# The spreading products of the norms, ranked 120 places later in a two-layer trunk

## The chip, the cores and the metric

The kernel runs as one program on one core of one Trainium2 chip. The metric is the device time of one execution in microseconds, the median of several runs. Before the change it is 2375.06 us (three runs, 2371.31 to 2375.71).

## What is computed

One step of a trunk of two layers over 1032 token columns (1024 of a prompt and 8 samples), width 1024, in float32. Layer 0 mixes by a gated recurrence and a causal convolution whose output has a LayerNorm of its own; layer 1 mixes by a short gated convolution. After every mixer and after every feed-forward block (width 2816) comes a post-norm:

```python
def _layernorm(x, w, b):
    mu = jnp.mean(xf, axis=-1, keepdims=True)
    var = jnp.mean(jnp.square(xf - mu), axis=-1, keepdims=True)
    return (xf - mu) * lax.rsqrt(var + LN_EPS) * w + b

# odd layer
p = x @ w_in                       # three parts bg, cg, xv
z = cg * xv
y = (bg * _causal_dwconv(z_ext, conv_w)) @ w_out
x = _layernorm(ALPHA * x + y)
# both layers
f = (silu(x @ w1) * (x @ w3)) @ w2
x = _layernorm(ALPHA * x + f)
```

## The kernel before

The channels lie on the partitions, the tokens along the free axis, in three chunks of 384, 384 and 264 columns (numbers 0, 1 and 2). A chunk's running state is `r` (eight slices of 128 channels). For the matrix products every operand is split in a high and a low part by `split` (L119 to L121): ScalarE casts the high part (L120), VectorE subtracts it from the source (L121). Weights come by SyncE's DMAs in units of 128 x 1024 (`raw`, 512 KB) and are split into `wh` and `wl`; activations are split into `x0ha, x0la, x0hb, x0lb` (chunk 0, slices 0 to 3 and 4 to 7), the same with `x1` for chunk 1, `x2h, x2l` for chunk 2, and `hb` for the hidden units of a feed-forward block. `mm` (L141 to L150) multiplies one unit by one chunk: for each of eight slices three matmuls (L147 `wl` by the high part, L148 `wh` by the low part, L149 `wh` by the high part) into one PSUM tile. They are called large matmuls here; they are nearly all of TensorE's work. Some projections of chunks 0 and 1 run through a scheme with fewer products (`project`), whose operands `t2`, `t3` are made on VectorE (L691 to L705).

A norm is the generator `normalise` (L220 to L270). It sums the slices on VectorE, spreads the mean by one TensorE product (L230), subtracts it (L241), squares on ScalarE (L248), sums (L250, L253), brings the sum of squares to the partitions by 4 or 3 small products with one column each (L256), scales it on VectorE (L201) and raises it to the power -0.5 on POOL (L202). This gives `rs`, one factor per token, with the tokens on the partitions. Then 4 (3 for chunk 2) small products spread it over all partitions (L265): `rs`, broadcast, by the identity, 96 columns each (88 for chunk 2), each in two passes in the profile. They write one tile of the PSUM pool `sm` (three buffers). VectorE multiplies the four pairs of slices by it (L268), and the affine step follows (L280 on VectorE for slice 0, L282 on ScalarE for the others), then the splits into `x?h`, `x?l`, which the next large matmuls read. The norm of the convolution in layer 0 goes the same way with two pairs and ends in L568 to L570 and in the splits of `x1` or `x2`.

There are 15 norms, in the order of the program: 1 the convolution of chunk 0; 2 the mixer's norm of chunk 0; 3 and 4 the convolutions of chunks 1 and 2; 5 and 6 the mixer's norms of chunks 1 and 2; 7, 8, 9 the feed-forward norms of layer 0 (chunks 0, 1, 2); 10, 11, 12 the mixer's norms of layer 1; 13, 14, 15 the final norms.

The order of each engine's instructions is set when the program is built, by a scheduler of tiles: an instruction takes the place that its number `tc.cur_priority` gives it. The number grows as the code is written, so that what is written later stands later, as far as dependences and buffers allow. The code raises or lowers the number by hand at a few places (`LATER = 1500` around the convolution, L556 to L559). On the chip each engine works through its fixed order and waits where an operand is not there.

Of the kernel before, what the change touches and what calls it, by code (L numbers as in the profile page):

```python
# [48 lines left out]
HC_BUFS = 24  # L49
TP_BUFS = 4  # L50
LATER = 1500
DVE_AFFINE = (0,)
DVE_AFFINE_LAST = (5, 6, 7)

# [14 lines left out]
def trunk(ctx: ExitStack, tc: tile.TileContext, xT, win0, wout0, win1, wout1, w1, w3, w2, vecs, sh, scf, ssc,  # L69
# [127 lines left out]
    def col(i):  # L197
        return vec[:, i:i + 1]

    def rsqrt_small(dst, src, scale, eps, n, p=P):  # L200
        VE.tensor_scalar(dst, src, scale, eps, ALU.mult, ALU.add)  # L201
        GP.tensor_tensor(dst, dst, mhalf[:p, :n], ALU.pow)  # L202
# [17 lines left out]
    def normalise(pairs, w, onesm, denom, last=False):  # L220


        acc = lnp.tile([P, 2, 384], F32, name="acc")
        mu = smp.tile([P, 512], F32, name="sm")[:, :w]
        n = len(pairs) - last
        VE.tensor_tensor(acc[:, :, :w], pairs[0], pairs[1], ALU.add)
        for v2 in pairs[2:n]:
            VE.tensor_tensor(acc[:, :, :w], acc[:, :, :w], v2, ALU.add)
        VE.tensor_tensor(acc[:, 0, :w], acc[:, 0, :w], acc[:, 1, :w], ALU.add)
        PE.matmul(mu, onesm, acc[:, 0, :w], start=True, stop=not last)  # L230
        if last:
            VE.tensor_tensor(acc[:, 1, :w], pairs[-1][:, 0], pairs[-1][:, 1], ALU.add)
            PE.matmul(mu, onesm, acc[:, 1, :w], start=False, stop=True)
        yield
        nb = 4 if w == 384 else 3
        bw = w // nb
        st = smp.tile([P, 512], F32, name="sm")
        rs = lnp.tile([P, 4], F32, name="rs")
        acc2 = lnp.tile([P, 2, 384], F32, name="acc")
        for j, v2 in enumerate(pairs):  # L240
            VE.tensor_tensor(v2, v2, mu.unsqueeze(1).broadcast_to([P, 2, w]), ALU.subtract)  # L241
            if j == 0:
                sq = acc2
            elif last and j == 2:
                sq = lnp.tile([P, 2, 384], F32, name="acc")
            else:
                sq = lnp.tile([P, 2, 384], F32, name="sq", bufs=1)
            SC.square(sq[:, :, :w], v2)  # L248
            if j and not last:
                VE.tensor_tensor(acc2[:, :, :w], acc2[:, :, :w], sq[:, :, :w], ALU.add)  # L250
            if last or j == len(pairs) - 1:
                z = sq if last else acc2
                VE.tensor_tensor(z[:, 0, :w], z[:, 0, :w], z[:, 1, :w], ALU.add)  # L253
                for i in range(nb):
                    k = 4 * i + j if last else i
                    PE.matmul(st[:bw, k:k + 1], z[:, 0, i * bw:(i + 1) * bw], ones, start=True, stop=True)  # L256
        var = st[:bw, :nb]
        if last:
            var = rs[:bw, :nb]
            VE.tensor_reduce(var, st[:bw, :4 * nb].rearrange("p (i j) -> p i j", j=4), mybir.AxisListType.X, ALU.add)  # L260
        rsqrt_small(rs[:bw, :nb], var, 1.0 / denom, LN_EPS, nb, bw)
        yield
        pb = smp.tile([P, 512], F32, name="sm")[:, :w]
        for i in range(nb):
            PE.matmul(pb[:, i * bw:(i + 1) * bw], rs[:bw, i:i + 1].broadcast_to([bw, P]), ident[:bw, :bw],  # L265
                      start=True, stop=True)
        for j, v2 in enumerate(pairs):
            VE.tensor_tensor(v2, v2, pb.unsqueeze(1).broadcast_to([P, 2, w]), ALU.mult)  # L268
            if j % 2:
                yield  # L270

    def layer_norm(c, wi, bi, out=None):
        a, b = CH[c]
        view = rc[c]
        last = out is not None and c == 2
        yield from normalise([view[:, j:j + 2, :] for j in range(0, NK, 2)], b - a, on1k, D, last)
        for k in range(NK):
            v = view[:, k, :]
            if k in (DVE_AFFINE_LAST if last else DVE_AFFINE):
                VE.tensor_scalar(v, v, col(wi + k), col(bi + k), ALU.mult, ALU.add)  # L280
            else:
                SC.activation(v, v, AF.Identity, bias=col(bi + k), scale=col(wi + k))  # L282
            if out is None:
                split(*xp(k, c), v)
            elif k % 2:
                nc.sync.dma_start(out[:, NK * a:NK * b].rearrange("p (k t) -> p k t", k=NK)[:, k - 1:k + 1, :],
                                  view[:, k - 1:k + 1, :])
            if k % 2:
                yield
# [47 lines left out]
    with tc.tile_pool(name="hg", bufs=1) as hg, tc.tile_pool(name="hg2", bufs=2) as hg2:  # L337
# [169 lines left out]
        def conv(i, gs, u, acc):  # L507

            w = sum(CH[g][1] - CH[g][0] for g in gs)
            W = w - NS if 2 in gs else w  # L510
            VE.tensor_scalar(acc[:, :w], u[:, 30:30 + w], col(V_DW + 30 * 4 + i), col(V_DWB + i), ALU.mult, ALU.add)
            for d in range(1, KW):
                lo = d if gs[0] == 0 else 0
                VE.scalar_tensor_tensor(acc[:, lo:W], u[:, 30 + lo - d:30 + W - d], col(V_DW + (30 - d) * 4 + i),  # L514
                                        acc[:, lo:W], ALU.mult, ALU.add)
            if 2 in gs:
                st = hg.tile([P, NS, 30], F32, name="stc", tag="vm")
                nc.sync.dma_start(st, scf[i])
                nw = hg.tile([P, NS, 30], F32, name="ncs", tag="S0t")
                SC.copy(nw[:, :, 0:29], st[:, :, 1:30])  # L520
                SC.copy(nw[:, :, 29], u[:, 30 + W:30 + W + NS])
                nc.sync.dma_start(cs_o[i], nw)
                nc.sync.dma_start(cp_o[i], u[:, W:W + 30])
                dw = vec[:, V_DW:V_DW + 120].rearrange("p (j i) -> p i j", i=4)[:, i, :]
                VE.tensor_tensor(st, st, dw.unsqueeze(1).broadcast_to([P, NS, 30]), ALU.mult)
                ts = hg.tile([P, NS], F32, name="tcs")
                VE.tensor_reduce(ts, st, mybir.AxisListType.X, ALU.add)
                VE.tensor_tensor(acc[:, W:W + NS], acc[:, W:W + NS], ts, ALU.add)

        def conv_units(i, gs):  # L530
# [25 lines left out]
            p = tc.cur_priority  # L556
            tc.cur_priority = p + LATER
            conv(i, gs, u_t, ctile[gs, i // 2][:, i % 2, :])
            tc.cur_priority = p  # L559

        def conv_finish(g):
            w = CH[g][1] - CH[g][0]
            pairs = [ctile[g, j] for j in range(2)]
            yield from normalise(pairs, w, on512, 512)
            for i in range(4):
                v = pairs[i // 2][:, i % 2, :]
                sg = hg2.tile([P, 384], F32, name="ct")[:, :w]
                SC.activation(sg, v, AF.Sigmoid, bias=col(V_CLB + i), scale=col(V_CLW + i))  # L568
                SC.activation(v, v, AF.Identity, bias=col(V_CLB + i), scale=col(V_CLW + i))
                VE.tensor_tensor(v, v, sg, ALU.mult)  # L570
                put_y(4 + i, g, v)
                if i % 2:
                    yield
# [247 lines left out]
    with tc.tile_pool(name="t0", bufs=1, reuse_waits="tile") as tp:  # L821
        F0.T = {j: t_pair(tp, j) for j in (2, 3)}
        with tc.tile_pool(name="head0", bufs=1, reuse_waits="tile") as act:
# [6 lines left out]
            for m in range(0, NEARLY, 4):  # L830
# [4 lines left out]
                p = tc.cur_priority  # L835
# [117 lines left out]
    with tc.tile_pool(name="t1", bufs=1, reuse_waits="tile") as tp:  # L953
        F1.T = {j: t_pair(tp, j) for j in (2, 3)}
        with tc.tile_pool(name="head1", bufs=1, reuse_waits="tile") as act:
# [12 lines left out]
            p = tc.cur_priority  # L968
# [81 lines left out]
```

## Time and profile before

| what | before |
|---|---|
| median of 3 runs | 2375.06 us (2371.31 to 2375.71) |
| the profiled execution | 2371.57 us |
| its span in the profile | 2369.5 us |
| TensorE busy | 2311.5 us, 98% |
| VectorE busy | 1789.8 us, 76% |
| ScalarE busy | 903.6 us, 38% |
| POOL busy | 42.8 us, 2% |

The span runs from the first to the last instruction; the execution is 2.1 us longer. TensorE's busy time counts overlapping, pipelined matmuls, so the distance between the starts of two matmuls says what one costs, and the length of a row does not. Where a row waited, the time and what released it stand in brackets.

### The profile page before, as it was taken

Reading aid. Unit: us, or ns where it says so; the run is one execution under the profiler, and the core shown is the slowest. Engines: PE = TensorE matmul, PEld = TensorE weight load, DVE = VectorE, ACT = ScalarE, POOL = GpSimd, SP = SyncE. Lnnn points to the kernel's source line nnn. Section 1 sums busy time; section 2 is a strip of 40 time slices with the busy share of each in tenths; the row PEclk is TensorE's granted clock in tenths of the full one; section 3 lists DMA queues with packets and bytes.
Section 4 is the critical chain, followed back from the end, with each engine's and each line's share of the span. In section 5 each row is a group of like instructions: output and inputs, shape, how many; then the busy total and the mean of one; then the engine's idle time right before and its main releaser. Section 6 shows DMA issues by size and latency. Waiting matters only on the chain.

```text
span 2369.5 us, 36483 instructions
## 1 busy us (share of the span) xinstructions
PE 2311.5 (98%) x14866; PEld 2272.3 (96%) x14866; DVE 1789.8 (76%) x2980; ACT 903.6 (38%) x1504; POOL 42.8 (2%) x40
## 2 busy tenths in 40 slices
PE   9999999999899999999999899999999999999997
PEld 8999999999899999999999899999999999999997
DVE  8998888787863336777788888877857777777775
ACT  5434353335631223332355333444513332332552
POOL 0000000000000000000000000000000000000000
PEclk9999999999999999999999999999999999999998
DMA  5322322343341221222442233434402222224651
GB/s 190 115 79 73 97 78 69 116 161 115 116 125 45 80 73 48 69 81 65 154 147 73 63 107 106 120 116 147 119 19 72 79 72 63 63 81 125 206 194 46
DMA packets 86999, 235.03 MB, mean 99 GB/s; under 512 B 8384, under 2 KB 26560, under 8 KB 86576
## 3 DMA queue, kind: packets, MB, share of 16 engines
q1 hardware_dynamic: 86672, 232.26, 32.0%
q8 instruction: 116, 1.90, 0.3%
q0 software_dynamic: 160, 0.45, 0.1%
q14 instruction: 51, 0.42, 0.1%
HBM read 225.46 MB, written 7.21 MB: 98 GB/s over the span
## 4 chain that ended last, share of the span: by engine, by line
PE 89%; DVE 6%; ACT 2%; POOL 1%; issue 1%; DMA 1%; SPq 0%; POOLq 0%; DVEq 0%; ACTq 0%
PE mm L147 20%; PE mm L149 20%; PE mm L148 20%; PE mm L656 8%; PE mm L657 8%; PE mm L655 8%; PE sm L368 2%; DVE wl L121 1%; DVE cc L514 1%; POOL rs L202 1%; PE sm L265 1%; ACT wh L120 1%; ACT r L282 0%; PE sm L415 0%; PE sm L397 0%
## 5 line engine op out<-in xcount | busy, mean ns | idle before, releaser
L120 ACT CAST wh<-raw 128x1024 fp32r<-128x1024 f32 (+1 forms) x494 | 493.3, 1001 | 898.2 <-PE mm L149 530.1
L121 DVE TENSOR_TENSOR wl<-raw,wh 128x1024 fp32r<-128x1024 f32 (+1 forms) x494 | 572.7, 1161 | 152.5 <-ACT wh L120 148.4
L147 PE MATMUL mm<-x2h,wl 128*128 128x264 f32 x1216 | 351.5, 289 | 20.5 <-DVE wl L121 20.5
L149 PE MATMUL mm<-x2h,wh 128*128 128x264 f32 x1216 | 349.6, 287 | 0.0
L148 PE MATMUL mm<-x2l,wh 128*128 128x264 f32 x1216 | 348.8, 287 | 0.0
L147 PEld LDWEIGHTS mm<-x2h,wl 128*128 128x128 f32 x1216 | 232.4, 191 | 23.0 <-DVE wl L121 22.6
L296 DVE TENSOR_TENSOR r<-r,mm 128x384 f32<-128x384 f32 (+1 forms) x336 | 171.2, 521 | 96.8 <-PE mm L149 96.2
L148 PEld LDWEIGHTS mm<-x2l,wh 128*128 128x128 f32 x1216 | 232.5, 191 | 0.3
L149 PEld LDWEIGHTS mm<-x2h,wh 128*128 128x128 f32 x1216 | 231.8, 191 | 0.8 <-issue 0.8
L147 PE MATMUL mm<-hb,wl 128*128 128x384 f32 (+1 forms) x672 | 211.1, 319 | 2.4 <-ACT hb L120 2.3
L148 PE MATMUL mm<-hb,wh 128*128 128x384 f32 (+1 forms) x672 | 213.2, 319 | 0.0
L149 PE MATMUL mm<-hb,wh 128*128 128x384 f32 (+1 forms) x672 | 212.3, 318 | 0.0
L514 DVE SCALAR_TENSOR_TENSOR cc<-r,vec,cc 128x640 f32<-128x640 f32 (+19 forms) x240 | 172.5, 737 | 1.2
L147 PEld LDWEIGHTS mm<-hb,wl 128*128 128x128 f32 x672 | 125.0, 188 | 4.7 <-ACT hb L120 4.7
L148 PEld LDWEIGHTS mm<-hb,wh 128*128 128x128 f32 x672 | 126.2, 188 | 0.5 <-DVE hb L121 0.2
L149 PEld LDWEIGHTS mm<-hb,wh 128*128 128x128 f32 x672 | 126.3, 188 | 0.3
L147 PE MATMUL mm<-x0ha,wl 128*128 128x384 f32 x312 | 108.3, 348 | 6.8 <-DVE wl L121 6.8
L148 PE MATMUL mm<-x0la,wh 128*128 128x384 f32 x312 | 108.0, 346 | 0.8 <-DVE x0la L121 0.8
L149 PE MATMUL mm<-x0ha,wh 128*128 128x384 f32 x312 | 108.5, 348 | 0.0
L149 PE MATMUL mm<-x0hb,wh 128*128 128x384 f32 x312 | 108.0, 346 | 0.0
L147 PE MATMUL mm<-x0hb,wl 128*128 128x384 f32 x312 | 107.4, 344 | 0.0
L148 PE MATMUL mm<-x0lb,wh 128*128 128x384 f32 x312 | 107.0, 343 | 0.0
(320 smaller groups left out, 5425.4 us busy)
## 6 DMA issues: line engine op xcount, KB each, us to landing
raw<-in_w SPq DMA_DIRECT2D x256, 512.0 KB, 3.6
raw<-in_win SPq DMA_DIRECT2D x98, 512.0 KB, 3.7
raw<-in_wout SPq DMA_DIRECT2D x48, 512.0 KB, 3.6
raw<-in_w SPq DMA_DIRECT2D x16, 256.0 KB, 2.6
out_yT<-r SPq DMA_DIRECT2D x8, 384.0 KB, 3.0
S0t<-in_sh SPq DMA_DIRECT2D x8, 256.0 KB, 3.4
out_hs<-S0t SPq DMA_DIRECT2D x8, 256.0 KB, 2.0
r<-in_xT SPq DMA_DIRECT2D x4, 384.0 KB, 6.7
```

Source lines behind the costliest of these rows:

```text
L120: SC.copy(hi, src)
L121: VE.tensor_tensor(lo, src, hi.bitcast(F32), ALU.subtract)
L147: PE.matmul(ps, wl[:, k, :], h, start=k == 0, stop=False)
L148: PE.matmul(ps, wh[:, k, :], l, start=False, stop=False)
L149: PE.matmul(ps, wh[:, k, :], h, start=False, stop=k == kt - 1)
L202: GP.tensor_tensor(dst, dst, mhalf[:p, :n], ALU.pow)
L296: VE.tensor_tensor(v, v, ps, ALU.add)
L368: PE.matmul(ps[:sr, c * 64:(c + 1) * 64].rearrange("p (b i) -> p b i", i=hh), kp[:, c * P:c * P + sr], qr, start=True, stop=True)
L514: VE.scalar_tensor_tensor(acc[:, lo:W], u[:, 30 + lo - d:30 + W - d], col(V_DW + (30 - d) * 4 + i), acc[:, lo:W], ALU.mult, ALU.add)
L655: PE.matmul(ps, w[1][:, k], t[0][:, k], start=k == 0, stop=False)
L656: PE.matmul(ps, w[0][:, k], t[1][:, k], start=False, stop=False)
L657: PE.matmul(ps, w[0][:, k], t[0][:, k], start=False, stop=k == 3)
```

## The change

The spreading products of L265 are ranked 120 places later than the code around them: the priority number is raised before the loop and set back after it. What follows them in the code (L268 and on) keeps its own number, but needs their result.

```diff
@@ constants
 LATER = 1500
+FACTOR_LATER = 120
@@ normalise
         rsqrt_small(rs[:bw, :nb], var, 1.0 / denom, LN_EPS, nb, bw)
         yield
         pb = smp.tile([P, 512], F32, name="sm")[:, :w]
+        p = tc.cur_priority
+        tc.cur_priority = p + FACTOR_LATER
         for i in range(nb):
             PE.matmul(pb[:, i * bw:(i + 1) * bw], rs[:bw, i:i + 1].broadcast_to([bw, P]), ident[:bw, :bw],
                       start=True, stop=True)
+        tc.cur_priority = p
         for j, v2 in enumerate(pairs):
             VE.tensor_tensor(v2, v2, pb.unsqueeze(1).broadcast_to([P, 2, w]), ALU.mult)
```

In the changed code the lines after the edit have other numbers: the spreading product is L268 there (L265 before), the multiplication L272 (L268), the variance product L257 (L256), the three large matmuls L148 to L150 (L147 to L149), the split L122 (L121).

The groups of norms 3, 4 and 7 to 14 (10 of 15, 37 products) stand elsewhere in TensorE's order; those of 1, 2, 5, 6 and 15 stay. Most lie 35 to 95 rows later, and single products now alternate with large matmuls, where a block of three or four stood before. POOL's order is the same. On VectorE the multiplications and splits that hang on the group stand later, behind weight splits and other work. On SyncE the load of a small state tile goes behind one more weight load, and the output transfers of norms 13 and 14 behind several.

TensorE around the variance and spreading products of norm 4 (convolution of chunk 2), before. `x1ha` to `x1lb` are chunk 1's operands:

```order
L256 MATMUL sm<-ones,acc 88x1 x3
L147 MATMUL mm<-x1ha,wl 128x384
L148 MATMUL mm<-x1la,wh 128x384
L149 MATMUL mm<-x1ha,wh 128x384
L147 MATMUL mm<-x1hb,wl 128x384
L148 MATMUL mm<-x1lb,wh 128x384
L149 MATMUL mm<-x1hb,wh 128x384
L147 MATMUL mm<-x1hb,wl 128x384
L148 MATMUL mm<-x1lb,wh 128x384
L265 MATMUL sm<-ident,rs 128x88 x3
```

And after the change:

```order
L257 MATMUL sm<-ones,acc 88x1 x3
L148 MATMUL mm<-x1ha,wl 128x384
L149 MATMUL mm<-x1la,wh 128x384
L150 MATMUL mm<-x1ha,wh 128x384
L268 MATMUL sm<-ident,rs 128x88
L148 MATMUL mm<-x1ha,wl 128x384
L268 MATMUL sm<-ident,rs 128x88
L149 MATMUL mm<-x1la,wh 128x384
L268 MATMUL sm<-ident,rs 128x88
L150 MATMUL mm<-x1ha,wh 128x384
```

Before, eight large matmuls stood between the variance products and the spreading products; now three do, since the variance products moved further than the spreading ones.

TensorE before the first products on chunk 2 after norm 12 (mixer's norm of chunk 2, layer 1), after the change. `x2h` is chunk 2's high operand, which that norm writes:

```order
L268 MATMUL sm<-ident,rs 128x88
L148 MATMUL mm<-x1hb,wl 128x384
L268 MATMUL sm<-ident,rs 128x88
L149 MATMUL mm<-x1lb,wh 128x384
L268 MATMUL sm<-ident,rs 128x88
L150 MATMUL mm<-x1hb,wh 128x384
L148 MATMUL mm<-x1hb,wl 128x384
L149 MATMUL mm<-x1lb,wh 128x384
L150 MATMUL mm<-x1hb,wh 128x384
L148 MATMUL mm<-x1hb,wl 128x384
L149 MATMUL mm<-x1lb,wh 128x384
L150 MATMUL mm<-x1hb,wh 128x384
```

Behind the last of these rows stands the first large matmul that reads `x2h`: nine large matmuls after the first spreading product. Before, the block of three stood 73 rows further from it.

VectorE at norm 9 (feed-forward norm of chunk 2, layer 0), where the mixer of layer 1 begins, before. `z` is the mixer's product, `r_74` the state of chunk 2:

```order
L897 TENSOR_TENSOR z_12308<-mm,z_12308 128x384
L268 TENSOR_TENSOR r_74<-r_74,sm 128x528
L873 TENSOR_SCALAR acc<-z_12308,vec 128x384
L268 TENSOR_TENSOR r_74<-r_74,sm 128x528
L876 SCALAR_TENSOR_TENSOR acc<-z_12308,vec,acc 128x384
L268 TENSOR_TENSOR r_74<-r_74,sm 128x528
L876 SCALAR_TENSOR_TENSOR acc<-z_12308,vec,acc 128x384
L268 TENSOR_TENSOR r_74<-r_74,sm 128x528
L280 TENSOR_SCALAR r_74<-r_74,vec 128x264
L904 TENSOR_TENSOR z_12300<-mm,acc 128x384
L121 TENSOR_TENSOR x2l<-r_74,x2h 128x264
```

And after the change:

```order
L908 TENSOR_TENSOR z_12300<-mm,acc 128x384
L695 TENSOR_TENSOR acc<-x1ha,x1la 128x768
L908 TENSOR_TENSOR z_12308<-mm,acc 128x384
L695 TENSOR_TENSOR acc<-x1hb,x1lb 128x768
L122 TENSOR_TENSOR wl<-raw,wh 128x1024
L704 TENSOR_TENSOR sq<-acc 128x768
L122 TENSOR_TENSOR t3l<-sq,t3h 128x768
L695 TENSOR_TENSOR sq<-x0ha,x0la 128x768
L708 TENSOR_TENSOR sq<-sq,acc 128x768
L709 SCALAR_TENSOR_TENSOR acc<-sq,acc 128x768
L272 TENSOR_TENSOR r_74<-r_74,sm 128x528 x4
```

The four multiplications stood ahead of the `z` products of L904 (L908 now); they now stand behind both of them, in one block.

## Rows read from the trace of the kernel before

**Rows 1.** The page's first part: busy time of each engine.
```profile
PE 2311.5 (98%) x14866; PEld 2272.3 (96%) x14866; DVE 1789.8 (76%) x2980; ACT 903.6 (38%) x1504; POOL 42.8 (2%) x40
```

**Rows 2.** The waits by line: total us, count, mean us.
```profile
PE sm L265 <- POOL rs L202: 10.4, 10, 2.1
```

**Rows 3.** TensorE timeline at norm 7: start us, length us, count.
```profile
1208.77 1.03 PE L265 MATMUL sm<-ident,rs 96*128 96x96 f32 x8
1209.58 0.37 PE L147 MATMUL mm<-x2h,wl 128*128 128x264 f32 x1
```

**Rows 4.** TensorE timeline at norms 3, 4, 8, 11, 12 and 14.
```profile
543.96 1.51 PE L265 MATMUL sm<-ident,rs 96*128 96x96 f32 x8 [2.12 <-POOL rs L202]
...
567.26 0.90 PE L265 MATMUL sm<-ident,rs 88*128 88x88 f32 x6 [0.61 <-POOL rs L202]
...
1243.83 0.28 PE L147 MATMUL mm<-x2h,wl 128*128 128x264 f32 x1
1244.97 1.13 PE L265 MATMUL sm<-ident,rs 96*128 96x96 f32 x8 [0.86 <-POOL rs L202]
1245.89 0.37 PE L148 MATMUL mm<-x2l,wh 128*128 128x264 f32 x1
...
1619.11 1.13 PE L265 MATMUL sm<-ident,rs 96*128 96x96 f32 x8 [0.23 <-POOL rs L202]
...
1668.23 0.90 PE L265 MATMUL sm<-ident,rs 88*128 88x88 f32 x6 [1.16 <-POOL rs L202]
...
2264.89 1.13 PE L265 MATMUL sm<-ident,rs 96*128 96x96 f32 x8 [0.86 <-POOL rs L202]
```

**Rows 5.** One stretch behind norm 3's wait: busy PE, PEld, DVE, ACT, POOL; PEclk, DMA.
```profile
544.00:547.50 3.50, 3.50 (x19) 3.50 (x20) 1.99 (x3) 0.00 (x0) 0.00 (x0) 0.58 0.51 150
```

**Rows 6.** TensorE timeline where small products already stand between large matmuls.
```profile
114.87 0.42 PE L147 MATMUL mm<-x0hb,wl 128*128 128x384 f32 x1
115.13 0.27 PE L502 MATMUL sm<-ident,o 128*128 128x128 f32 x1
115.16 0.42 PE L148 MATMUL mm<-x0lb,wh 128*128 128x384 f32 x1
...
222.27 0.29 PE L149 MATMUL mm<-x2h,wh 128*128 128x264 f32 x1
...
222.80 0.39 PE L147 MATMUL mm<-x2h,wl 128*128 128x264 f32 x1
```

**Rows 7.** TensorE timeline at large matmuls that read what the norms and splits write.
```profile
553.99 0.34 PE L148 MATMUL mm<-x1lb,wh 128*128 128x384 f32 x1
...
1256.38 0.39 PE L147 MATMUL mm<-hb,wl 128*128 128x264 f32 x1 [0.19 <-ACT hb L120]
...
1336.39 0.59 PE L147 MATMUL mm<-x2h,wl 128*128 128x264 f32 x1 [9.18 <-DVE wl L121]
...
1633.41 0.39 PE L147 MATMUL mm<-x2h,wl 128*128 128x264 f32 x1 [0.51 <-DVE wl L121]
...
1681.93 0.34 PE L149 MATMUL mm<-x1hb,wh 128*128 128x384 f32 x1
1682.11 0.28 PE L147 MATMUL mm<-x2h,wl 128*128 128x264 f32 x1
1682.23 0.28 PE L148 MATMUL mm<-x2l,wh 128*128 128x264 f32 x1
```

**Rows 8.** VectorE timeline at norms 3, 8, 9 and 12.
```profile
553.18 1.02 DVE L121 TENSOR_TENSOR x1lb<-cc,x1hb 128x384 fp32r<-128x384 f32 x2
...
1246.14 3.55 DVE L268 TENSOR_TENSOR r<-r,sm 128x768 f32<-128x768 f32 x4 [2.09 <-PE sm L265]
...
1278.80 0.56 DVE L897 TENSOR_TENSOR z<-mm,z 128x384 f32<-128x384 f32 x1 [2.31 <-PE mm L149]
...
1287.79 0.56 DVE L904 TENSOR_TENSOR z<-mm,acc 128x384 f32<-128x384 f32 x1 [0.23 <-PE mm L149]
...
1669.17 2.55 DVE L268 TENSOR_TENSOR r<-r,sm 128x528 f32<-128x528 f32 x4 [1.70 <-PE sm L265]
```

## The prediction

> **What bounds the kernel now.** I read the page's busy times first. TensorE is busy 98% of the span, VectorE 76%, ScalarE 38%, POOL 2% [rows 1]: TensorE sets the time, and only what changes the distance between its matmuls counts. The waits by line come next. The spreading products wait for POOL's factor `rs` 10 times over all fifteen norms, 10.4 us in the sum as this view counts it [rows 2]; which norms these are, and what each is worth, has to come from the timeline. Then the timeline, group by group. At norm 7 the block of four products (eight passes) costs 0.81 us from its start to the next large matmul and waits for nothing [rows 3], 0.20 per product. Six of the ten groups that move do wait: norms 3, 4, 8, 11, 12 and 14, for 2.12, 0.61, 0.86, 0.23, 1.16 and 0.86 us [rows 4], together 5.84. A wait costs more than it shows: at norm 8 the large matmuls on both sides of the block start 2.06 us apart; less their own 0.12 (chunk 2's distance, 1682.11 to 1682.23 [rows 7]), 0.81 for the block and 0.86 for the wait, 0.27 is left. So the change can take away at most 5.84 + 6 x 0.27 = 7.5 us of waits. Behind the wait of norm 3 the granted clock was 0.58 in the 3.50 us that follow [rows 5], between the levels of 1.2 and 2.4 GHz, with TensorE busy throughout; at full clock that work takes 3.50 x 0.58 = 2.0 us, so 1.4 us more hang on this wait. Upper end of the gain: 8.9 us.
>
> **The price of a later factor.** What the norm writes comes later too, and each stage has a reader. The question at each group is whether TensorE meets the output earlier than it is there.
>
> Norm 3: the wait of 2.12 + 0.27 goes, and the slow clock with it (1.4), as the spreading products go behind 21 large matmuls that need no factor. But the product on `x1lb` at 553.99 [rows 7] stands only 0.3 us behind the first of the two splits that write it (553.18, two of 0.5 each [rows 8]). Its chain begins with the same factor at about the same time: TensorE arrives 3.8 earlier and the data only some 1.6 (a ScalarE cast of `x2h` no longer waits for the slow matmuls in front). Net -1.6.
>
> Norm 4: in the order, three large matmuls are left between the variance products and the spreading products, where eight were. Eight at 0.17 (chunk 1's distance, 1681.93 to 1682.11 [rows 7]) are 1.4; they and the 0.61 wait were the length of the chain over VectorE and POOL, 2.0. Three cover 0.5: a wait of 1.5 in place of 0.61, +0.9, less a little since the variance products came later themselves and find their sums ready (I take 0.5 back). Net +0.4.
>
> Norm 8: 0.86 + 0.27 goes. In return, the multiplications (3.55 for four [rows 8]) and three more splits of `x1la` (0.5 each) stand ahead of the last `hb` of the feed-forward block. TensorE had no lead there: it waited 0.19 for that `hb` already [rows 7]. The three splits and 0.5 for the group's own spread give 2.0. Net +0.9. Norm 7 goes the same way without a wait to save; bounds 0 and 3.55, I take 1.0, nearer to nothing since no row shows TensorE waiting there.
>
> Norm 9: VectorE bounds this stage; TensorE waits 9.18 us for the split weights at its end (1336.39 [rows 7]). Before, VectorE used its waits for TensorE (2.31 at 1278.80, 0.23 at 1287.79 [rows 8]) with the four multiplications in between. The order now puts them behind both `z` products. So the four multiplications of 0.64 each, 2.55 in all (the chunk 2 form of norm 12 [rows 8]) no longer lie in idle time, and VectorE has them to do later, inside the stretch that TensorE waits for. Bounds 0 and 2.55; the wait of 9.18 says that VectorE has no slack, so I take 2.5.
>
> Norm 10: no wait before, the multiplications go ahead of a weight split that TensorE wants soon after; bounds 0 and 3.55, I take 1.0, as at norm 7. Norm 11: 0.23 + 0.27 goes, and the wait of 0.51 on a weight split at 1633.41 [rows 7] shows that TensorE has no lead behind it: half of the 3.55 of multiplications, 1.8, comes back. Net +1.3.
>
> Norm 12: 1.16 + 0.27 goes. In the order nine large matmuls (9 x 0.17 = 1.6 us) are left between the first spreading product and the first reader of `x2h`. Between the spreading products and the reader were 13.9 us before (1668.23 to 1682.11 [rows 4, 7]). The chain takes 0.94 to the first multiplication (1668.23 to 1669.17 [rows 4, 8]), 2.55 for four of them, and some 0.6 for the affine step and the split: 4.1. So a wait of 2.5 takes the place of 1.43. Net +1.1.
>
> Norm 13: no wait and no early reader, 0. Norm 14: 0.86 + 0.27 goes, and only the output hangs on it. Net -1.1.
>
> The products themselves, now one by one between large matmuls (33 of 37): where a transpose already stands so, two large matmuls start 0.29 apart instead of 0.17, 0.12 for one pass (114.87 to 115.16) [rows 6]. A spreading product has two passes; a second pass in the block costs 0.10. So 0.22 against 0.20, 33 x 0.02 = +0.7. Bounds: the large matmul follows the small one by 0.03 (115.13 to 115.16) [rows 6], so 0.06 for two passes, 33 x 0.14 = -4.6; and a pair of passes at 222.27 to 222.80 [rows 6] costs 0.53 less 0.12, 0.41, 33 x 0.21 = +6.9. That pair includes some wait. I take the near value. The Trainium skill ("TensorE: Matmul & The Clock Gate", "Step-by-step: what each phase is for") says that TensorE pulls the load of the next stationary operand ahead while the matmul in front still runs. By that rule a small product between large ones hides its load and this term would be the lower bound, -4.6, in place of +0.7; the 0.12 per pass at 114.87 does not agree with it.
>
> SyncE's moved transfers (a small tile behind one more weight load; outputs of norms 13 and 14 behind several) have no reader on TensorE: 0, up to one weight load's delay if a unit came late. POOL keeps its order: 0.
>
> **The sum.** -1.6 + 0.4 + 1.0 + 0.9 + 2.5 + 1.0 + 1.3 + 1.1 + 0 - 1.1 + 0.7 = +6.2 us. On the profiled execution's 2371.57 that is 2377.8. That execution lies 3.5 below the median of 2375.06, so my forecast for the median is 2381.3. About 0.2% (4.75 us) is what a measurement of this kernel can tell from no change.
>
> **Rivals.**
> 1. The saved waits carry through and the outputs have slack: 8.9 saved, only norm 9's 2.5 paid: 2375.06 - 6.4 = 2368.7, faster. For it: six waits go with certainty from where they stood [rows 4]. Against it: `x1lb` and `hb` are met with 0.3 us to spare or less [rows 7, 8]. It decides at whether TensorE meets `x1lb`, `hb`, the weight splits and `x2h` before they are written. Chance 0.24.
> 2. Savings and later waits cancel: the waits move from the spreading products to the readers of the norm, the sum near 0, 2375. For it: the factor itself comes no later, so a chain that TensorE waits out has the same length. Chance 0.22.
> 3. A small product between large ones costs 0.41, the upper bound of rows 6, at 33 places, beside the waits cancelling: +6.9, and with half of my sum's waits 2385. Against it: 0.12 per pass at 114.87. Chance 0.13.
> 4. A small product between large ones is nearly free: its load hides, -4.6 - 0.7 on my sum: 2376.0. For it, the 0.03 us at 115.13 [rows 6]; against it, the same place shows 0.12 between the large ones. That is what the rule of the Trainium skill above would make of it. Chance 0.08.
> That the change does nothing is excluded by the order: 10 of 15 groups stand elsewhere.
>
> **How the numbers follow.** My forecast has 0.33, its own range 2377 to 2387: I count 0.29 as slower by over 0.2% (above 2379.8) and 0.04 as same. With rival 3 slower is 0.42; with rivals 2 and 4 same is 0.34; rival 1 makes faster 0.24. The range for 8 in 10 runs from just below rival 1, 2368, to 2390, where the ends of norms 7 and 10 (3.55 each instead of 1.0) put my sum (2381.3 + 5.1, and some of the pairs' bound). What lies outside is all six waits saved with nothing paid, and the full +6.9 on top of my sum.
>
> **What the changed profile would show.** Right: the waits for `rs` at norms 3, 8, 11, 12 and 14 gone, one of about 1.5 at norm 4; a new wait of TensorE on `x2h` of about 2.5 before the first product of chunk 2 behind norm 12; the wait on `hb` near 1256 grown to about 2; the wait on the weight split near 1336 grown from 9.2 to nearly 12; the granted clock full behind norm 3; large matmuls around a spreading product some 0.4 apart. Wrong: none of these readers waits, and TensorE's time is shorter by the sum of the waits (rival 1); or the large matmuls around each spreading product are 0.6 apart (rival 3) or 0.25 (rival 4).

## The result and the profile after

The changed kernel takes 2396.09 us (median of 4 runs, 2392.16 to 2398.30) against 2375.09 us: ratio 1.0089, 95% interval 1.0077 to 1.0101, slower by 21 us. The forecast was 2381.3 with a range up to 2390: the sign held, the size was a third of it. The profiled execution took 2392.16 us with a span of 2390.1, so its span is 20.6 longer than that of before, and it lies 3.9 below its median as the one of before lies 3.5 below its own.

The page's busy times, answering to [rows 1]:

```profile
PE 2320.8 (97%) x14866; PEld 2278.5 (95%) x14866; DVE 1790.7 (75%) x2980; ACT 902.6 (38%) x1504; POOL 45.4 (2%) x40
```

The number of instructions is the same and VectorE's work is too. TensorE is busy 9.3 us longer with the same matmuls, and idle 11.3 us longer. Both parts have to be explained, and they have one cause.

Both programs hold 13,668 large matmuls, in nearly the same order. So I compare the start of the k-th one in both traces and let the difference grow along the program. Idle is what TensorE stood still in that stretch; the rest is the same work taking longer.

| stretch (us of before) | longer by | of it idle | rest |
|---|---|---|---|
| start to 540 (same order) | +2.1 | +0.4 | +1.7 |
| 540 to 556, norm 3 | -2.7 | -1.1 | -1.7 |
| 556 to 571, norm 4 | +7.3 | +3.4 | +3.9 |
| 571 to 1207 (norms 5 and 6) | -0.2 | -0.1 | -0.1 |
| 1207 to 1241, norm 7 | +1.5 | +1.1 | +0.4 |
| 1241 to 1266, norm 8 | +2.2 | +1.8 | +0.4 |
| 1266 to 1347, norm 9 and the mixer | +4.2 | +1.3 | +2.9 |
| 1381 to 1581 (no moved group) | -0.5 | 0.0 | -0.5 |
| 1581 to 1611, norm 10 | +1.0 | +1.0 | -0.1 |
| 1611 to 1645, norm 11 | +3.5 | +2.2 | +1.3 |
| 1645 to 1687, norm 12 | +4.6 | +1.7 | +2.9 |
| 1687 to 2228 (no moved group) | -1.5 | 0.0 | -1.5 |
| 2228 to 2281, norms 13 and 14 | -1.5 | -0.9 | -0.6 |

The waits are first to be read in TensorE's timeline of the changed kernel, beside [rows 4, 7] (start, length, what it waited for in brackets):

```profile
548.08 0.35 PE L268 MATMUL sm<-ident,rs 96*128 96x96 f32 x1 [1.06 <-POOL rs L203]
565.13 0.32 PE L257 MATMUL sm<-ones,acc 128*88 128x1 f32 x2 [0.99 <-DVE acc L254]
566.26 0.44 PE L148 MATMUL mm<-x1ha,wl 128*128 128x384 f32 x1 [0.50 <-DVE wl L122]
569.30 0.51 PE L268 MATMUL sm<-ident,rs 88*128 88x88 f32 x1 [2.26 <-POOL rs L203]
1248.18 0.39 PE L148 MATMUL mm<-x2h,wl 128*128 128x264 f32 x1 [1.08 <-DVE wl L122]
1264.62 0.39 PE L148 MATMUL mm<-hb,wl 128*128 128x264 f32 x1 [1.50 <-DVE hb L327]
1265.97 0.39 PE L148 MATMUL mm<-hb,wl 128*128 128x264 f32 x1 [0.71 <-ACT hb L121]
1329.47 0.56 PE L148 MATMUL mm<-x2h,wl 128*128 128x264 f32 x1 [5.86 <-DVE wl L122]
1344.68 0.59 PE L148 MATMUL mm<-x2h,wl 128*128 128x264 f32 x1 [4.63 <-DVE wl L122]
1617.14 0.41 PE L148 MATMUL mm<-x0ha,wl 128*128 128x384 f32 x1 [1.04 <-DVE wl L122]
1653.70 0.43 PE L148 MATMUL mm<-x2h,wl 128*128 128x264 f32 x1 [2.92 <-DVE wl L122]
1702.60 0.81 PE L148 MATMUL mm<-x2h,wl 128*128 128x264 f32 x2 [2.80 <-ACT x2h L121]
```

The waits for `rs` at norms 8, 11, 12 and 14 are gone, that of norm 3 is halved, and one of 2.26 has come at norm 4. In their place stand waits on what the norms write or hold up: `hb`, split weights, `x2h`. The forecast named these places. The second half is in the granted clock behind them (stretches of the changed kernel: length, busy TensorE and count, PEclk, DMA share, GB/s):

```profile
569.00:575.00 6.00, 5.70 (x20) 0.50 0.48 186
1329.50:1332.50 3.00, 3.00 (x14) 0.50 0.61 169
1344.70:1350.00 5.30, 5.30 (x24) 0.50 0.32 99
1653.70:1657.00 3.30, 3.30 (x15) 0.53 0.61 160
1702.60:1708.40 5.80, 5.75 (x24) 0.50 0.32 90
```

Behind each of the five waits of 2.2 us or more in this list TensorE works for 3 to 6 us at 0.50 to 0.53, that is at 1.2 GHz and not 2.4, with matmuls in every us of it. At full clock this work would be done in half the time, so 11.6 us are lost in these five stretches (6.0, 3.0, 5.3 and 5.8 x 0.50, 3.3 x 0.47). Before, two of the places had such a loss: behind norm 3's wait 1.4 to 1.8 [rows 5], and behind the wait of 9.18 [rows 7], here:

```profile
1336.40:1341.00 4.60, 4.60 (x25) 0.62 0.00 0
```

4.6 x 0.38 is 1.7. So some 8 of the 21 us are the clock (11.6 less the 1.4 to 1.8 and the 1.7), and 11.3 the waits themselves; about 1 us is in neither sum. The granted clock averaged over whole executions agrees: 0.985 over the four of the changed kernel, 0.988 to 0.989 over the 99 of the kernel before that ran beside the experiments. By these means an execution spends some 70 us instead of 53 to 56 at the lower level. Half of the difference is lost, an estimate of 7 to 9 us.

VectorE at norm 9, beside [rows 8]: with the four multiplications gone from between them, the two `z` products wait for TensorE (0.76 and 2.68, where the second waited 0.23 before and the first not at all).

```profile
1293.71 0.56 DVE L908 TENSOR_TENSOR z<-mm,acc 128x384 f32<-128x384 f32 x1 [0.76 <-PE mm L150]
...
1297.94 0.56 DVE L908 TENSOR_TENSOR z<-mm,acc 128x384 f32<-128x384 f32 x1 [2.68 <-PE mm L150]
```

And the price of a product that stands alone (norm 7, beside [rows 3]):

```profile
1226.19 0.28 PE L150 MATMUL mm<-x2h,wh 128*128 128x264 f32 x1
1226.31 0.36 PE L268 MATMUL sm<-ident,rs 96*128 96x96 f32 x2
1226.45 0.37 PE L148 MATMUL mm<-x2h,wl 128*128 128x264 f32 x1
1226.65 0.36 PE L268 MATMUL sm<-ident,rs 96*128 96x96 f32 x2
1226.80 0.37 PE L149 MATMUL mm<-x2l,wh 128*128 128x264 f32 x1
```

Between the large ones the first product adds 0.14 (1226.19 to 1226.45, less 0.12) and each further one 0.22 to 0.23: 0.14 + 3 x 0.225 = 0.82 for four, where the block cost 0.81. The large matmul behind the last product is 0.08 slow in both orders. Alternating costs nothing.

### The profile page after: what moved, and what is told of

The parts are those of the page before. It is cut to its first block, busy times and chain, and to the rows that moved or that the text cites. A ratio compares the mean times of both kernels' runs of the same rounds, so it can differ in the third digit from the quotient of the medians.

```text
span 2390.1 us, 36490 instructions
## 1 busy us (share of the span) xinstructions
PE 2320.8 (97%) x14866; PEld 2278.5 (95%) x14866; DVE 1790.7 (75%) x2980; ACT 902.6 (38%) x1504; POOL 45.4 (2%) x40
## 4 chain that ended last, share of the span: by engine, by line
PE 90%; DVE 5%; ACT 2%; DMA 1%; POOL 1%; issue 1%; SPq 0%; POOLq 0%; DVEq 0%; ACTq 0%
PE mm L148 21%; PE mm L150 21%; PE mm L149 21%; PE mm L660 8%; PE mm L661 8%; PE mm L659 8%; PE sm L372 2%; DVE wl L122 1%; DVE cc L518 1%; PE sm L268 1%; ACT r L286 1%; POOL rs L203 0%; PE sm L419 0%; PE sm L231 0%; PE sm L452 0%
## 5 line engine op out<-in xcount | busy, mean ns | idle before, releaser
L121 ACT CAST wh<-raw 128x1024 fp32r<-128x1024 f32 (+1 forms) x494 | 493.6, 1001 | 901.2 <-PE mm L150 536.1
L122 DVE TENSOR_TENSOR wl<-raw,wh 128x1024 fp32r<-128x1024 f32 (+1 forms) x494 | 572.3, 1161 | 170.8 <-ACT wh L121 166.5
L148 PE MATMUL mm<-x2h,wl 128*128 128x264 f32 x1216 | 353.6, 291 | 28.1 <-DVE wl L122 25.3
L150 PE MATMUL mm<-x2h,wh 128*128 128x264 f32 x1216 | 350.7, 289 | 0.0
L149 PE MATMUL mm<-x2l,wh 128*128 128x264 f32 x1216 | 350.1, 288 | 0.0
L148 PEld LDWEIGHTS mm<-x2h,wl 128*128 128x128 f32 x1216 | 234.1, 193 | 31.7 <-DVE wl L122 22.1
L149 PEld LDWEIGHTS mm<-x2l,wh 128*128 128x128 f32 x1216 | 234.1, 193 | 0.3
L150 PEld LDWEIGHTS mm<-x2h,wh 128*128 128x128 f32 x1216 | 233.2, 192 | 0.8 <-issue 0.8
L148 PE MATMUL mm<-hb,wl 128*128 128x384 f32 (+1 forms) x672 | 210.9, 320 | 4.9 <-ACT hb L121 2.8
L149 PE MATMUL mm<-hb,wh 128*128 128x384 f32 (+1 forms) x672 | 212.2, 318 | 0.2 <-DVE hb L122 0.2
L150 PE MATMUL mm<-hb,wh 128*128 128x384 f32 (+1 forms) x672 | 211.7, 317 | 0.0
L148 PEld LDWEIGHTS mm<-hb,wl 128*128 128x128 f32 x672 | 124.8, 188 | 7.5 <-ACT hb L121 5.0
L149 PEld LDWEIGHTS mm<-hb,wh 128*128 128x128 f32 x672 | 126.1, 188 | 0.9 <-DVE hb L122 0.7
L150 PEld LDWEIGHTS mm<-hb,wh 128*128 128x128 f32 x672 | 126.1, 188 | 0.0
L148 PE MATMUL mm<-x0ha,wl 128*128 128x384 f32 x312 | 108.0, 347 | 8.3 <-DVE wl L122 8.3
L149 PE MATMUL mm<-x0la,wh 128*128 128x384 f32 x312 | 107.4, 344 | 0.7 <-DVE x0la L122 0.7
L148 PE MATMUL mm<-x1ha,wl 128*128 128x384 f32 x312 | 107.4, 344 | 0.6 <-DVE wl L122 0.5
L150 PE MATMUL mm<-x0ha,wh 128*128 128x384 f32 x312 | 107.9, 346 | 0.0
L150 PE MATMUL mm<-x0hb,wh 128*128 128x384 f32 x312 | 107.4, 344 | 0.0
L149 PE MATMUL mm<-x1lb,wh 128*128 128x384 f32 x312 | 107.3, 344 | 0.0
```

The costliest lines, as they stand in the source:

```text
L121: SC.copy(hi, src)
L122: VE.tensor_tensor(lo, src, hi.bitcast(F32), ALU.subtract)
L148: PE.matmul(ps, wl[:, k, :], h, start=k == 0, stop=False)
L149: PE.matmul(ps, wh[:, k, :], l, start=False, stop=False)
L150: PE.matmul(ps, wh[:, k, :], h, start=False, stop=k == kt - 1)
```

## Experiments

Each is the changed kernel with another table of places (norm: places later, 0 for a norm that isn't in it); a counter numbers the norms as in the text. Single lines of the edits are shown, "..." marks what is left out. The kernel before ran beside them: 2374.49 us beside the first four, 2373.9 beside the next three and the one with "just some rows", 2373.35 beside the 40 places, the groups that gained and the five fillings, 2373.95 beside the two fillings.

```diff
-FACTOR_LATER = 120
+FACTOR_LATER = {3: 120}
...
-    steps = []
+    steps = []; norm_no = [0]
...
-        p = tc.cur_priority
-        tc.cur_priority = p + FACTOR_LATER
+        p = tc.cur_priority; norm_no[0] += 1
+        tc.cur_priority = p + FACTOR_LATER.get(norm_no[0], 0)
```

**One part of the change at a time.** Norm 3 alone ({3: 120}; norm 4's group and its variance products shift along):

> Only norm 3's spreading products are ranked later (norm 4's group and its variance products shift with them, as in the changed kernel). Theory A (each moved group has its own price: the next reader waits, and TensorE runs at the lower clock behind that wait; the prices add up): about +4.6 us on before, the sum that the two traces differ by between the matmuls at 540 and 571 us; the wait at norm 3 falls from 2.1 to about 1.1, one of 2.3 or more appears at norm 4, and the granted clock there is about 0.6 for some microseconds. Rival B (the price sits in the spreading products themselves, 21 us over 37 products, wherever they stand): 7 products, +4.0, with no particular place. Rival C (the forecast's own terms, without any clock): -1.2.

2377.32 us (ratio 1.0011, 1.0002 to 1.0020), +2.8. In the trace norm 3's stretch gains 2.7 and norm 4's loses 5.0; the wait at norm 4 is smaller than in the changed kernel, where norm 4's own group was ranked later as well:

```profile
570.42 0.90 PE L268 MATMUL sm<-ident,rs 88*128 88x88 f32 x6 [1.29 <-POOL rs L203]
```

So theory A had the places and was 2.3 too high, since it took both edits for one.

Norms 7 and 8 ({7: 120, 8: 120}):

> Only norms 7 and 8 are ranked later. Theory A: +3.8 us on before (1.5 around norm 7, 2.2 around norm 8), shown as new waits of TensorE of 1.1 for split weights and of 1.5 and 0.7 for hb, no loss of clock. Rival B: 8 products, +4.5. Rival C: +1.9.

2378.50 us (1.0013, 1.0004 to 1.0022), +4.0; the stretches give 1.5 and 3.1. The waits are 1.08, 1.50 and 0.71, the same three as in the changed kernel. But behind the last the clock falls here, against theory A, where the changed kernel's profile has 1.00 from 1264.6 to 1270; that makes most of the difference between 3.1 and 2.2. It is not the order that decides it: the filled kernel below (norm 12 filled, the same order here as in the changed kernel) has the lower clock at this place too, and its stretch is 3.0.

```profile
1257.40:1262.00 4.60, 4.40 (x22) 0.66 0.42 128
```

Norm 9 ({9: 120}):

> Only norm 9 is ranked later, three products. Theory A: +4.2 us on before: VectorE stands idle some 2.7 us longer for the mixer's first products, TensorE's one wait of 9.2 for split weights becomes two of about 5, and the granted clock falls behind both instead of one. Rival B: 3 products, +1.7. Rival C: +2.5.

2377.25 us (1.0011, 1.0002 to 1.0020), +2.8; the stretch gives 4.2. The two waits and the clock behind them are nearly those of the changed kernel:

```profile
1319.13 0.56 PE L148 MATMUL mm<-x2h,wl 128*128 128x264 f32 x1 [5.86 <-DVE wl L122]
1334.34 0.59 PE L148 MATMUL mm<-x2h,wl 128*128 128x264 f32 x1 [4.93 <-DVE wl L122]
```

```profile
1319.10:1322.10 3.00, 2.97 (x13) 0.50 0.55 175
1334.30:1339.60 5.30, 5.26 (x25) 0.54 0.34 99
```

Norms 10, 11 and 12 ({10: 120, 11: 120, 12: 120}):

> Only norms 10, 11 and 12 are ranked later, eleven products. Theory A: +9.1 us on before (1.0, 3.5 and 4.6), with waits of about 1.0 (split weights), 2.9 (split weights) and 2.8 (x2h), and the granted clock down behind the last two. Rival B: 11 products, +6.2. Rival C: +3.4.

2381.59 us (1.0030, 1.0018 to 1.0041), +7.1; the stretches give 0.9, 3.5 and 4.9, with waits of 0.99, 2.92 and 2.80.

Norms 13 and 14 ({13: 120, 14: 120}):

> Only norms 13 and 14 are ranked later, eight products. Theory A: -1.5 us on before (0.3 and 1.2): the wait of 0.86 at norm 14 goes, and only the output hangs on these norms. Rival B: 8 products, +4.5. Rival C: -1.1.

2372.78 us (0.9993, 0.9982 to 1.0003), -1.1; the stretches give -0.3 and -1.2. Rival B wants +4.5 here and is out: the price isn't in the products. The five timed parts sum to 15.6 us, the change is 21.0. Their stretches sum to 18.8 (2.3, 4.6, 4.2, 9.2, -1.5), and 2.3 more come where norms 3 and 4 are moved together. So the traces add up to the change. The timed parts fall short of it by 5.4, of which the traces give 2.3 to norms 3 and 4 together; each of the five has an interval of 2 to 3 us to either side, as the change has, so the remaining 3 are within the noise of the sum.

**The wait at norm 4.** Norm 4 at 130 places ({3: 120, 4: 130}), so that more large matmuls stand ahead of its spreading products:

> Norm 3 ranked 120 places later and norm 4 130 places, so that 11 more large matmuls stand between norm 4's variance products and its spreading products than with norm 3 alone. Theory A: the wait of about 2.3 and the lower clock at norm 4 go, and the stretch of both convolution norms costs about 1 us or less on before instead of 4.6. If the price at norm 4 came from the lateness of what it writes, the time would be that of norm 3 alone or above it.

2375.82 us (1.0010, 1.0000 to 1.0020), +1.9. The wait for `rs` falls to 0.38, and the clock in the 5 us behind it is 0.96, where norm 3 alone had 0.66:

```profile
571.04 0.61 PE L268 MATMUL sm<-ident,rs 88*128 88x88 f32 x2 [0.38 <-POOL rs L203]
```

The distance to the variance products made that wait. But the stretch still costs about 1.2 (norms 3 and 4 together, less than with norm 3 alone, more than the 1 expected): the variance products still wait 0.99 for their sum, since TensorE comes earlier after norm 3, the large matmul behind them waits 0.51, and behind these two, ahead of the wait for `rs`, the clock is 0.50 from 568 to 571.

**The clock by itself.** The changed kernel, with 14 products of constants that nobody reads put in the wait behind norm 12:

```diff
+FILL = {12: (133, 14)}
...
+        norm_no[0] += 1
+        if norm_no[0] in FILL:
+            later, count = FILL[norm_no[0]]
+            tc.cur_priority = p + later
+            spare = smp.tile([P, 512], F32, name="sm")
+            for _ in range(count):
+                PE.matmul(spare[:, :P], on1k, on1k, start=True, stop=True)
         tc.cur_priority = p
```

> The changed kernel with 14 more small products of constants (128 columns, read by nobody) directly ahead of the first reader of x2h behind norm 12, where TensorE waits 2.8 us. Theory A: they fit in the wait, the x2h products start at the same distance as in the changed kernel, and at full clock: about 2.9 us less than the changed kernel, near 2393. If the lower clock does not come from the wait, or if it costs nothing, the time stays at that of the changed kernel or rises by up to 2.5.

2393.26 us (1.0075, 1.0060 to 1.0090), 2.8 below the changed kernel's median with more work to do; the intervals of the two ratios overlap, so the trace has to decide:

```profile
1702.74 3.29 PE L277 MATMUL sm<-on1k 128*128 128x128 f32 x28
1705.78 0.49 PE L149 MATMUL mm<-x2h,wl 128*128 128x264 f32 x2
```

```profile
1702.60:1705.80 3.20, 3.20 (x31) 1.00 0.24 96
1705.80:1711.60 5.80, 5.53 (x42) 1.00 0.27 90
```

The products fill the wait, the first reader of `x2h` starts 3.0 us after their begin, where it waited 2.80 in the changed kernel, and the 5.8 us behind are granted 1.00, not 0.50. The stretch of norm 12 costs 1.9 less than in the changed kernel. One profile at one place could be chance, so the fillings below count too: of eight filled waits none has the lower clock behind it, where the unfilled waits of 2.1 to 3.6 us at norm 3 and near 615, 1168 and 2188 us have it in 40 of 47 cases over all profiles. That the lower clock comes from TensorE standing still, and that it is a price beside the wait, is shown by them together.

**How far later.** All norms, but 40 places:

> All norms as in the changed kernel, but ranked 40 places later and not 120. Norms 3 and 4 stay where they were, norms 8, 11, 12 and 14 move by 5 to 13 rows, norms 7, 9 and 13 by about 30; at norm 9 the multiplications stand between the two z products and not behind both. Theory A (the price is what the readers wait, and it grows with the distance): between -2 and +3 us on before; -2 if no reader waits longer, +3 if norm 9 pays half of its 4.2 and norm 7 its 1.5. Rival B (price per product that is taken out of its block): 21 products of the ten groups now stand alone, so +10 or more.

2376.54 us (1.0012, 1.0004 to 1.0021), +3.2: norm 12 gains 1.2, norm 8 loses 0.9, norm 9 1.8, the others nothing. Norm 9 keeps a single wait, of 10.67 for 9.18, and so pays the clock once:

```profile
1339.37 0.59 PE L148 MATMUL mm<-x2h,wl 128*128 128x264 f32 x1 [10.67 <-DVE wl L122]
```

At a third of the distance the change costs a seventh. In the trace 14 products stand alone, not the 21 expected; at 21 us over 37 products rival B makes that 8, and it is out again.

Only norms with a wait, by just some rows ({8: 80, 11: 70, 12: 45, 14: 80}):

> Only norms 8, 11, 12 and 14 are ranked later, and by less (80, 70, 45 and 80 places), so that the spreading products stand 6 to 15 large matmuls later and not 40 to 75. Theory A: the waits of 0.86, 0.23, 1.16 and 0.86 go, with 0.27 each, and most readers still meet their data: -2 to -4 us on before. If any lateness is paid in full by a reader, 0 or above.

2375.13 us (1.0003, 0.9992 to 1.0014): no gain. Norms 12 and 14 save 1.0 and 1.1; norm 8 costs 0.9, and at norm 11 the 0.7 saved is more than paid back by a wait of 1.66 on a weight split (0.51 before): +0.4.

**A better kernel.** Only the groups that gained ({12: 45, 13: 120, 14: 120}):

> Only the groups that gained: norm 12 by 45 places, norms 13 and 14 by 120. Theory A: -1.0 -0.3 -1.2 = -2.5 us on before.

2373.36 us against 2373.35 (0.9994, 0.9985 to 1.0003). The stretches show the -1.0, -0.3 and -1.2, the runs cannot tell it from no change. Then with fillings in five waits (`FILL_MM` gives the number of products ahead of a certain call of `mm`), the products being written to the PSUM tile that the waiting matmul then starts anew:

```diff
+        for _ in range(FILL_MM.get(mm_no[0], 0)):
+            PE.matmul(ps[:, :P], on1k, on1k, start=True, stop=True)
         for k in range(kt):
```

> The same, and small products of constants that nobody reads (128 columns) put where TensorE waits anyway: 11 ahead of norm 3's spreading products, 14 each ahead of the large matmuls that wait 3.62, 3.32 and 3.32 us for split weights at 615, 1168 and 2188 us, and 40 ahead of the one that waits 9.18 at 1336. Theory A (behind a wait of 2 us or more TensorE runs at the lower clock for some microseconds, 1.4 to 2.9 us lost each time, and filling the wait keeps the clock): five times 1.4 to 2 us, -7 to -10 beside the -2.5, so about 2363 to 2366. If the lower clock is not due to the waits: the time of the kernel without them, or more.

2371.16 us (0.9991, 0.9981 to 1.0000): a miss. Behind all five the clock stays at 1.00, and the stretches at 615, 1168, 1336 and 2188 are 1.4, 2.4, 1.5 and 2.4 shorter than before. Over its 12 executions the mean granted clock is 0.993, against 0.989 for the kernel before. But the order that the scheduler makes around norms 7 and 8 changed. The filling at 1168 stands closest ahead of that place; it was not tried by itself. In the profiled execution (2378.93, the slowest of the 12) the new order cost 8.9 between 1207 and 1250, by waits such as these:

```profile
1244.45 0.39 PE L154 MATMUL mm<-hb,wl 128*128 128x264 f32 x1 [2.12 <-DVE wl L124]
...
1259.84 0.39 PE L154 MATMUL mm<-x2h,wl 128*128 128x264 f32 x1 [2.12 <-DVE wl L124]
```

With two fillings only, those at 1336 and 2188, which leave that order alone:

> Norms 12, 13 and 14 later as in the kernel of the groups that gained, and only two of the five fillings: 40 small products where TensorE waits 9.18 us at 1336, and 14 where it waits 3.32 at 2188. These two leave the order up to norm 13 as it is; the filling at 1168 had changed the order around norms 7 and 8, which cost 8.9 us there. Theory A: -2.7 and -2.3 by the clock, +0.7 around norm 13, so 4 us below the kernel of the groups that gained, about 2369. If the fillings only save what their own products cost: the same time as that kernel, 2373.

2368.98 us against 2373.95 (0.9977, 0.9967 to 0.9987): 5 us faster than before, 27 faster than the changed kernel, as theory A said. Over its nine executions the mean granted clock is 0.991. The wait of 9.18 is filled, and the stretch behind it is at full clock, where the kernel without fillings (second line) has 0.50:

```profile
1328.76 9.09 PE L151 MATMUL mm<-on1k 128*128 128x128 f32 x80
1338.11 0.39 PE L154 MATMUL mm<-x2h,wl 128*128 128x264 f32 x1 [0.25 <-DVE wl L124]
```

```profile
1336.50:1341.00 4.50, 4.25 (x36) 1.00 0.00 0
1336.50:1341.00 4.50, 4.50 (x22) 0.50 0.20 24
```

## Why the prediction was wrong in size

| term | forecast | trace |
|---|---|---|
| norm 3 | -1.6 | -2.7 |
| norm 4 | +0.4 | +7.3 |
| norms 7, 8 | +1.0, +0.9 | +1.5, +2.2 |
| norm 9 | +2.5 | +4.2 |
| norm 10 | +1.0 | +1.0 |
| norm 11 | +1.3 | +3.5 |
| norm 12 | +1.1 | +4.6 |
| norms 13, 14 | 0, -1.1 | -0.3, -1.2 |
| alternating | +0.7 | 0.0 |
| sum | +6.2 | +20.1 |

The mechanism was the forecast's: the waits moved from the spreading products to the readers, at the places named, and the readers had no slack. Two things in the sum failed.

**The clock was counted on one side only.** The step at norm 3 took 1.4 us of lower clock as a gain when a wait of 2.1 goes, from [rows 5]. The steps at norms 4, 9, 11 and 12 put new waits of 1.5 to 2.5 in and gave them no such price. The same row would have said 1.4 behind a wait of 2.1. Measured, the clock is 3.0 of norm 4's 7.3, 2.4 of norm 9's 4.2 (1.5 and 2.65 behind its two waits, less the 1.7 of before), 1.5 of norm 11's 3.5 and 2.9 of norm 12's 4.6. Together they are 9.8 of the 13.9 us by which the sum was short. The filled wait shows it for norm 12.

**Some waits were sized too small.** Norm 12's wait was put at 2.5 and is 2.80; norm 9's longer idling of VectorE at 2.5, and is 3.2 in these two rows (0.5 less by a shorter wait ahead of them). These were near. But at norm 9 that idling did not reach TensorE whole: its waits grew only from 9.18 to 5.86 + 4.63 = 10.49, by 1.3 and not by 2.5, and the 4.2 of that stretch is for the larger part the clock. Norm 4's wait was put at 1.5 for `rs`; it is 2.26, and the variance products and the large matmul behind them wait 0.99 and 0.50 in addition, which I had put as a gain of 0.5. TensorE came 2.7 us earlier from norm 3, so that whatever stood close behind, VectorE's sum too, was late. Norm 11's return was taken as half of the multiplications, 1.8; the wait on the split grew from 0.51 to 2.92. At norm 3 two errors of opposite sign nearly met: the wait for `rs` was to go and is halved, and `x1lb` was to be met too early and is met without a wait (554.34 in the changed kernel), so that 2.7 were gained and not 1.6.

Rival 1 (outputs have slack) fell at the places where it was to be decided, and rival 2 (savings and later waits cancel) with the 11.3 us that TensorE stands idle longer. Rival 3 (0.41 for a product between large ones) and rival 4 (nearly free) are both out by 0.22 against 0.20. The rule of the Trainium skill on pulled-ahead weight loads ("TensorE: Matmul & The Clock Gate", "Step-by-step: what each phase is for") did not make the products cheap: only the first of a group adds less, 0.14, and whether a hidden load is the reason no run shows.

The range ended at 2390, because its upper end was built from more waiting in front of readers and not from the clock behind each wait.

## To carry to other kernels

In this kernel, a product that was moved later on the bounding engine only moved the wait to the first reader of its result, unless that reader was far: follow the chain to the reader before counting the wait as saved. If the profile shows the clock lower behind one wait, every new wait of that length has to be given the same price, as a likely one: a single execution may not pay it. And where a wait can't be removed, products that nobody reads can keep the clock up through it, as all eight filled waits here did, as long as they don't disturb the order around.

## Not expected

The lower clock behind a wait could cost as much as the wait itself or more: 2.9 us behind 2.80 at norm 12, 3.0 behind 2.26 at norm 4. At norms 9 and 11 it cost less than the wait (1.5 behind 5.86, 1.5 behind 2.92).

It does not come every time. The waits that no edit touched show this over the profiles of all fourteen kernels: behind the 5.2 us near 1530 the clock fell in 14 of 14, behind the 3.3 near 1168 in 12 of 13, behind the 3.3 near 2188 in 9 of 12 (not in the changed kernel's), behind the 1.27 at norm 6 in 8 of 14, behind the two of 1.07 near 1145 and 2165 in none of 28. The new waits of about 1 us at norms 7 and 10 had no such loss either; at norm 8, where two stand close together, it came in two profiles of three.

The clock also falls in stretches where both kernels have the same order: in the changed kernel's profile it is 0.55 from 453 to 460, where the profile of before has 1.00 in its 453 to 460, and that stretch alone is 3 us longer.

```profile
453.00:460.00 7.00, 7.00 (x21) 0.55 0.40 123
```

In the profiles of the twelve experiments, whose instructions up to 540 us stand in the same order, the stretch from 450 to 540 is longer than before by 2.2 to 3.0 us in four, by 1.0 and 1.3 in two, and by less than 0.5 either way in six. Single executions of this kernel therefore differ by some us for a reason that no edit made; what starts it was not tried.
